# Even layer, tokens 512-1023: index scores, pooling, query rotation and attention placed beside the MLP of tokens 0-511, with raw projections kept until then

## The chip, the core and the metric

The kernel runs on one core of a Trainium2 chip. The metric is the device time in microseconds (us) of one execution; lower is better. The engines named below are TensorE (PE, the matmuls), VectorE (DVE), ScalarE (ACT), GpSimd (POOL) and SyncE (SP, which issues the DMAs).

## What is computed

Two layers over 1024 tokens of width 1024, in float32, and a final norm. The even layer mixes sparse attention (an indexer picks 256 causal keys for each query) with a pooling mixer; the odd layer is a gated delta rule. Each layer ends in a squared-ReLU MLP with 4096 hidden columns.

```python
for layer in range(2):
    hn = rmsnorm(h, mix_norm[layer])
    h = h + (sparse_pool_mixer(hn, ...) if layer % 2 == 0 else gated_deltanet(hn, ...))
    h = h + squared_relu_mlp(rmsnorm(h, mlp_norm[layer]), w_ff1[layer], w_ff2[layer])
return rmsnorm(h, final_norm)

def sparse_pool_mixer(h, ...):
    q, c_kv, qi, ki, wi, u = jnp.split(h @ w_in, ...)
    # q, qi, k, ki are rotated (rope); c_kv is normed; k = c_kv @ w_uk; v = c_kv @ w_uv
    ya = dsa_attention(q, k, v, qi, ki, wi)          # score = sum_h relu(qi . ki) * wi; top_k(score, 256)
    yb = multiscale_pool(u, pool_w, pool_scale)      # trailing means over 2, 4, 8, 16 tokens, minus the token
    return jnp.concatenate([ya, yb], axis=-1) @ w_out

def squared_relu_mlp(h, w1, w2):
    return jnp.square(jax.nn.relu(h @ w1)) @ w2
```

## The kernel before

Activations lie transposed in SBUF (128 channels by 512 tokens a tile), so the 1024 tokens are two halves, s = 0 and s = 1. The residual of half s is `h[s]`, eight tiles. A float32 product is made of three matmuls (`mm3`) on a high and a low part of each operand: every weight chunk (128 x 512) is loaded by SP into a `raw` buffer, copied by ACT to its high part (`copy`) and subtracted by POOL to its low part (`rest`). A chunk feeds 12 matmuls of 512 columns. The parts lie in rings of buffers, `W` (6 buffers before, that is three chunks) and `WM` (4); `room` says which rings a stream of chunks uses and how many chunks are prepared ahead. Stream "a" is the layers' projections, stream "m" the MLPs.

The program is written as Python generators and then ordered by a scheduler: each engine has one queue in program order, in which `high_priority(offset=n)` moves instructions forward.

The even layer (`even`) runs through these stages. First the projections of half 0 (`EVEN_A`: latent keys `ckv`, index keys `kiwi`, index queries `qi`, pooling `u`, queries `q`), with index scores, pooling and rotation right behind each (`late` generators). Then the projections of half 1 (`EVEN_B`), with attention of half 0 (`attend`, query blocks 0 to 3) and the index scores of half 1 (`index_scores`, blocks 4 to 7) taken in turns. Then the output projection of half 0 (`even_out`), the four query projections of half 1 and the norm of `h[0]` for its MLP (`normed`).

From there the MLP of half 0 is available as a filler: `mlp_half` is a generator whose steps are one up-projection (`project`, 24 matmuls, then `squared`) or one row of the down-projection (`accumulate`, 6 matmuls and one DVE addition to `h`). A group of 256 hidden columns is two of the first and eight of the second, 96 matmuls. `EARLY = 63` such steps are placed beside the selection of half 1, by `more(2)` per step of `topk`; the rest runs alone later (`alone`).

`topk` finds the 256th largest score of each query by 31 steps of bisection on the bits, four blocks at once. In a step DVE counts for blocks 4 and 5 (`L625`), ACT for blocks 6 and 7 (`L652`), and three small DVE instructions (`L664`, `L665`, `L650`) set the next candidate. Afterwards each block gets its mask (`L632`, `L625`, `L688` to `L693`, with a scan, `L690`, that writes to the ring `temps`). `attend` then makes, per block and pair of heads, scores on PE (`L364`), maximum on DVE (`L705`), exponentials on ACT, transposes on PE (`L726`), copies of these by DVE and ACT (`L728`) and the product with the values on PE (`L735`).

After attention of half 1 and `even_out(1)` the rest of the MLP of half 0 runs alone. The odd layer follows, and needs `h[0]` complete. The lines with a helper's number stand for many places: `L246` to `L248` are all `mm3`, `L175` all high parts, `L179` all low parts.

Of the kernel before, what the change touches and what calls it, by code (L numbers as in the profile page):

```python
# [34 lines left out]
EARLY = 63  # L35
# [99 lines left out]
class Trunk:  # L135
    def __init__(self, ctx, tc, I, out):
# [13 lines left out]
        self.H = [Ring(mp, f"h{n}", 8, 512) for n in range(2)]  # L150
        self.background, self.masked, self.pace, self.solo = [], {0, 1}, 3, False
# [75 lines left out]


# [307 lines left out]

    def even_query(self, s, p, ps):

        pc = self.swapped(ps)
        yield  # L540
        self.qs[s].append(self.query_stacks(pc, s, self.Q))

    def even_pool(self, s, g, ps):
# [9 lines left out]
        nc.vector.tensor_tensor(u[:, 16:528], ps, self.rb, op=OP.mult)  # L553
# [10 lines left out]
        pl = self.H[1].get()  # L564
# [16 lines left out]
    def even_steps(self, s, x, keys, first=()):  # L581
# [21 lines left out]
    def topk(self, blocks, nv):  # L603
# [29 lines left out]

        for g in range(G):
# [14 lines left out]
        for b in range(30, -1, -1):  # L649
# [16 lines left out]
            yield  # L666
        for g in range(G):
# [131 lines left out]
    def squared(self, ps, ring):  # L799

        nc = self.nc
        r, y = self.T.get(), ring.parts()
# [3 lines left out]
        nc.vector.scalar_tensor_tensor(ps, ps, 0.0, r, op0=OP.max, op1=OP.mult)  # L806
        self.rest(y[:, 512:1024], ps, y[:, 0:512], False)
# [21 lines left out]
    def mlp_half(self, l, s, x, ring):  # L829
# [5 lines left out]
        for g, n, before, chunks in self.mlp_order():  # L835
            if g is not None:
                ps = self.project(("f1", l, 2 * g + n), x, st="m")
                if n == 0:
                    a[g] = [self.squared(ps, ring)]
# [3 lines left out]
            if g is not None and n == 1:  # L843
                a[g].append(self.squared(ps, ring))
# [342 lines left out]
    def even_units(self):  # L1187
# [11 lines left out]
        second = EVEN_B.copy()  # L1199
        second.insert(second.index(("u", 0)) + 3, "pool")  # L1200
        return list(chain(*(u[k] for k in first + second))) + out + list(chain(*(u["q", p] for p in range(4)))) + out


    def even(self):
# [3 lines left out]
        with ExitStack() as st:  # L1208
# [12 lines left out]
            with ExitStack() as st3:  # L1221
# [18 lines left out]
                scores = chain(*(self.index_scores(1, p) for p in range(4)))  # L1240
                for _ in self.even_steps(1, x, EVEN_B):
                    take(att, 3)
                    take(scores)
                while self.late:
                    take(att, 3)
                    take(scores)
                    self.step_late()
                for _ in att:
                    take(scores)
                acc, done = None, 0  # L1250
                for _ in self.even_out(0, ya, self.yb[0], self.PB):
# [3 lines left out]
                    take(scores)  # L1255
                self.x0 = self.rb
                self.room("a", self.W)
                for n, _ in enumerate(self.even_steps(1, x, [("q", p) for p in range(4)])):
                    if n == 0:
                        acc = self.rstd_cols(acc, D)  # L1260
                    if n == 1:
                        self.copy(self.x0, self.over_partitions(acc))
                    if n == 3:
                        self.x0 = self.normed(self.h[0], R_MLP, self.x0)
                        break
# [164 lines left out]
```

## Time and profile before

| | |
|---|---|
| median of 3 runs | 2830.18 us (2829.31 to 2831.47) |
| profiled execution | 2833.8 us |
| its span, first to last instruction | 2832.0 us |
| PE busy | 2652.9 us (94%) |
| DVE busy | 1711.8 us (60%) |
| mean granted TensorE clock | 0.972 of full speed |

The span is what the profile shows; the profiled execution's own time is 1.8 us longer. Busy time is an average over the whole program; the stages differ.

### The profile page before, as it was taken

Reading aid. Unit: us, or ns where it says so; the run is one execution under the profiler, and the core shown is the slowest. Engines: PE = TensorE matmul, PEld = TensorE weight load, DVE = VectorE, ACT = ScalarE, POOL = GpSimd, SP = SyncE. Lnnn points to the kernel's source line nnn. Section 1 sums busy time; section 2 is a strip of 40 time slices with the busy share of each in tenths; the row PEclk is TensorE's granted clock in tenths of the full one; section 3 lists DMA queues with packets and bytes.
Section 4 is the critical chain, followed back from the end, with each engine's and each line's share of the span. In section 5 each row is a group of like instructions: output and inputs, shape, how many; then the busy total and the mean of one; then the engine's idle time right before and its main releaser. Section 6 shows DMA issues by size and latency. Waiting matters only on the chain. (4 is left out here: it accounts for less than half of the span.)

```text
span 2832.0 us, 44713 instructions
## 1 busy us (share of the span) xinstructions
PE 2652.9 (94%) x16648; PEld 2097.5 (74%) x16648; DVE 1711.8 (60%) x3657; ACT 1186.2 (42%) x2472; POOL 1240.4 (44%) x1070
## 2 busy tenths in 40 slices
PE   8878969979999899999999989899999999899998
PEld 6656747857788677787777767677777777688886
DVE  6898898475533546565665567755665644733334
ACT  4556767345333343343333344433433323433332
POOL 6653354401544444445444434444444434544442
PEclk9889979989999999999999999999999999999999
DMA  5221123300332222222222211122222222333332
GB/s 165 65 67 45 59 84 95 92 12 23 101 97 89 80 78 78 69 71 83 79 72 76 70 53 56 55 78 68 75 79 79 66 63 86 117 98 96 96 96 78
DMA packets 119916, 218.81 MB, mean 77 GB/s; under 512 B 13970, under 2 KB 15122, under 8 KB 119698
## 3 DMA queue, kind: packets, MB, share of 16 engines
q1 hardware_dynamic: 119698, 215.95, 24.7%
q8 instruction: 131, 2.15, 0.3%
q14 instruction: 87, 0.71, 0.1%
HBM read 207.51 MB, written 4.19 MB: 75 GB/s over the span
## 5 line engine op out<-in xcount | busy, mean ns | idle before, releaser
L179 POOL TENSOR_TENSOR wm<-raw,wm 128x512 fp32r<-128x512 f32 x422 | 557.3, 1322 | 798.3 <-ACT wm L175 780.4
L175 ACT ACTIVATE wm<-raw 128x512 fp32r<-128x512 f32 x422 | 264.9, 628 | 654.4 <-PE ps_g L247 319.0
L179 POOL TENSOR_TENSOR w<-raw,w 128x512 fp32r<-128x512 f32 x222 | 295.9, 1334 | 345.5 <-ACT w L175 316.8
L820 DVE TENSOR_TENSOR h<-ps_d,h 128x512 f32<-128x512 f32 x424 | 288.0, 684 | 140.9 <-PE ps_d L248 139.2
L806 DVE SCALAR_TENSOR_TENSOR ps_g<-ps_g,temps 128x512 f32<-128x512 f32 x128 | 89.2, 696 | 358.8 <-ACT temps L804 358.8
L246 PE MATMUL ps_g<-x,w 128*128 128x512 f32 x644 | 260.7, 405 | 9.0 <-ACT w L175 6.3
L247 PE MATMUL ps_g<-x,w 128*128 128x512 f32 x644 | 260.0, 404 | 9.3 <-POOL x L179 6.0
L246 PE MATMUL ps_d<-y,wm 128*128 128x512 f32 x628 | 257.7, 410 | 11.3 <-DVE h L820 10.0
L248 PE MATMUL ps_g<-x,w 128*128 128x512 f32 x644 | 259.0, 402 | 0.7 <-POOL w L179 0.7
L175 ACT ACTIVATE w<-raw 128x512 fp32r<-128x512 f32 x222 | 138.9, 627 | 288.0 <-PE ps_g L247 191.2
L248 PE MATMUL ps_d<-y,wm 128*128 128x512 f32 x628 | 249.9, 398 | 0.6 <-POOL wm L179 0.6
L247 PE MATMUL ps_d<-y,wm 128*128 128x512 f32 x628 | 250.4, 399 | 0.0
L246 PE MATMUL ps_g<-xb,wm 128*128 128x512 f32 x512 | 205.2, 401 | 12.1 <-DVE y L179 7.6
L248 PE MATMUL ps_g<-xb,wm 128*128 128x512 f32 x512 | 205.3, 401 | 10.1 <-POOL wm L179 9.9
L247 PE MATMUL ps_g<-xb,wm 128*128 128x512 f32 x512 | 204.3, 399 | 0.6 <-POOL xb L179 0.6
L925 DVE SCALAR_TENSOR_TENSOR qkvz<-temps,conv,qkvz 128x512 f32<-128x512 f32 x144 | 134.8, 936 | 105.0 <-ACT qkvz L923 103.8
L246 PE MATMUL ps_g<-x,wm 128*128 128x512 f32 x352 | 142.1, 404 | 19.5 <-ACT x L175 15.4
L246 PEld LDWEIGHTS ps_g<-x,w 128*128 128x128 f32 x644 | 123.7, 192 | 40.7 <-ACT w L175 6.3
L247 PEld LDWEIGHTS ps_g<-x,w 128*128 128x128 f32 x644 | 123.8, 192 | 39.6 <-POOL x L179 7.5
L246 PEld LDWEIGHTS ps_d<-y,wm 128*128 128x128 f32 x628 | 118.3, 188 | 41.9 <-DVE h L820 14.5
L248 PEld LDWEIGHTS ps_g<-x,w 128*128 128x128 f32 x644 | 123.6, 192 | 28.2 <-POOL w L179 1.8
L247 PE MATMUL ps_g<-x,wm 128*128 128x512 f32 x352 | 142.0, 404 | 1.8 <-DVE x L179 1.2
(430 smaller groups left out, 6108.2 us busy)
## 6 DMA issues: line engine op xcount, KB each, us to landing
raw<-in_w_dram SPq DMA_DIRECT2D x512, 256.0 KB, 2.6
raw<-in_woi_dram SPq DMA_DIRECT2D x128, 256.0 KB, 2.6
raw<-in_wei_dram SPq DMA_DIRECT2D x52, 256.0 KB, 2.8
raw<-in_weo_dram SPq DMA_DIRECT2D x32, 256.0 KB, 2.6
raw<-in_woo_dram SPq DMA_DIRECT2D x32, 256.0 KB, 2.7
h<-in_xt_dram SPq DMA_DIRECT2D x16, 256.0 KB, 3.2
at<-at SPq DMA_DIRECT2D x64, 64.0 KB, 2.0
out_dram<-temps SPq DMA_DIRECT2D x16, 256.0 KB, 2.2
```

The costliest lines, as they stand in the source:

```text
L175: self.nc.scalar.activation(out, in_, AF.Copy)
L179: eng.tensor_tensor(lo, full, hi.bitcast(F32), op=OP.subtract)
L246: mm(ps, wh, xh, start=start, stop=False)
L247: mm(ps, wh, xl, start=False, stop=False)
L248: mm(ps, wl, xh, start=False, stop=stop)
L806: nc.vector.scalar_tensor_tensor(ps, ps, 0.0, r, op0=OP.max, op1=OP.mult)
L820: nc.vector.tensor_tensor(h, ps, h, op=OP.add)
L925: nc.vector.scalar_tensor_tensor(acc, pin[:, j:j + 512], cw(j), acc, op0=OP.mult, op1=OP.add)
```

## The change

Half 1's projections are all made right behind one another. The pooling and query projections of half 1 are only copied out of PSUM to the ring `H[1]` (`even_kept`). Two of them (`HELD = 2`, q2 and q3) are made behind `even_out(0)`. Then the norm of `h[0]` follows and the MLP of half 0 starts. Beside it stand, in this order, the 16 steps of the index scores of half 1, pooling and rotation on the kept tiles, the steps of `topk`, and the attention of half 1. `beside(us)` hands out MLP steps by a nominal budget per step: `BESIDE` is 4.0 (scores), 3.4 (kept tiles and bisection), 2.2 (attention), 6.0 (masks). Its unit is that of `T_COLS = 5.6` and `T_ROWS = 1.4` per MLP step.

Smaller edits: `W` has 4 buffers instead of 6, a ring `wo` of 2 serves the odd layer's output weights, and from `even_out(0)` on stream "a" uses `W` alone with one chunk ahead. The scan of a mask writes to `junk2` instead of a `temps` buffer. `topk` has its priority only while it searches. All four instructions of `squared` have priority 100 (before, the two on ACT). Half 1's pooling multiplies on POOL instead of DVE.

```diff
 KEYS = ["ckv", "kiwi"] + [("qi", p) for p in range(4)]
-EVEN_B = KEYS[:2] + list(chain(*((("u", p), ("qi", p)) for p in range(4))))
+EVEN_B = KEYS + [("u", p) for p in range(4)] + [("q", p) for p in range(4)]
+HELD = 2
+BESIDE = (4.0, 3.4, 2.2, 6.0)
...
-        self.W, self.WM, self.raw = Ring(wp, "w", 6, 512), Ring(wp, "wm", 4, 512), Ring(wp, "raw", 4, 512)
+        self.W, self.WM, self.raw = Ring(wp, "w", 4, 512), Ring(wp, "wm", 4, 512), Ring(wp, "raw", 4, 512)
...
-    @urgent(50)
     def step_background(self, g):
-        return next(g, self)
+        with self.tc.high_priority(offset=50) if self.searching else nullcontext():
+            return next(g, self)
...
+    def even_kept(self, s, key, ps):
+
+        raw = self.H[1].get()
+        self.copy(raw, ps)
+        self.kept.append((key, raw))
+        yield
+
...
-        nc.vector.tensor_tensor(u[:, 16:528], ps, self.rb, op=OP.mult)
+        (g2 if s else nc.vector).tensor_tensor(u[:, 16:528], ps, self.rb, op=OP.mult)
...
-            g = late[name](s, *n, ps)
+            g = self.even_kept(s, key, ps) if s and name in "uq" else late[name](s, *n, ps)
...
-            eq, cum = junk[:, :n], self.T.get(U16, n)
+            eq, cum = junk[:, :n], junk2.bitcast(U16)[:, :n]
...
             nc.scalar.activation(r, ps, AF.Relu)
             nc.scalar.activation(y[:, 0:512], r, AF.Square)
-        nc.vector.scalar_tensor_tensor(ps, ps, 0.0, r, op0=OP.max, op1=OP.mult)
-        self.rest(y[:, 512:1024], ps, y[:, 0:512], False)
+            nc.vector.scalar_tensor_tensor(ps, ps, 0.0, r, op0=OP.max, op1=OP.mult)
+            self.rest(y[:, 512:1024], ps, y[:, 0:512], False)
...
-                scores = chain(*(self.index_scores(1, p) for p in range(4)))
-                for _ in self.even_steps(1, x, EVEN_B):
+                for _ in self.even_steps(1, x, EVEN_B[:-HELD]):
                     take(att, 3)
-                    take(scores)
-                while self.late:
-                    take(att, 3)
-                    take(scores)
+                for _ in att:
                     self.step_late()
-                for _ in att:
-                    take(scores)
+                self.room("a", self.W)
...
+                for _ in self.even_steps(1, x, EVEN_B[-HELD:]):
                     pass
+                x0 = self.normed(self.h[0], R_MLP, r)
+
+                self.act = self.PB
+                fill, due = self.mlp_half(0, 0, x0), 0.0
+
+                def beside(us):
+                    nonlocal due
+                    due += us
+                    while due > 0:
+                        due -= next(fill)
+
+                for p in range(4):
+                    for _ in self.index_scores(1, p):
+                        beside(BESIDE[0])
+                for (name, n), raw in self.kept:
+                    g = {"u": self.even_pool, "q": self.even_query}[name](1, n, raw)
+                    next(g)
+                    self.step_late()
+                    self.late.append(g)
+                    beside(BESIDE[1])
+                    self.tick(1)
+                while self.late:
+                    beside(BESIDE[1])
+                    self.tick(1)
+                    self.step_late()
...
-            more(12)
             while self.background:
-                more(2)
+                beside(BESIDE[1] if self.searching else BESIDE[3])
                 self.tick(1)
+            beside(BESIDE[3])
...
-                for _ in self.attend(range(4, 8), self.qs[1], pb, ya):
-                    more(2)
-                more(EARLY)
+                att = self.attend(range(4, 8), self.qs[1], pb, ya)
+
+                with self.tc.issue_after(self.last_matmul()):
+                    next(att)
+                for _ in att:
+                    beside(BESIDE[2])
...
-            self.room("o", self.W, ahead=0)
+            self.room("o", Ring(op, "wo", 2, 512), ahead=0)
```

Three places show what the scheduler makes of it. The line numbers are those of the kernel in question; most lines of the changed kernel stand a few numbers lower or higher.

First DVE in the bisection, one up-projection's stretch of it. Before (`L664` sets the bit, `L806` and `L179` are `squared`, `L820` is a row's addition to `h`):

```order
L664 TENSOR_TENSOR tk_keep<-tk_cnt,tk_top 128x4
L665 COPY_PREDICATED tk_cur<-tk_keep,tk_cand 128x4
L650 TENSOR_SCALAR tk_cand<-tk_cur 128x4
L806 SCALAR_TENSOR_TENSOR ps_g<-ps_g,temps 128x512
L820 TENSOR_TENSOR h_101<-ps_t,h_101 128x512
L179 TENSOR_TENSOR y<-ps_g,y 128x512
L820 TENSOR_TENSOR h_102<-ps_t,h_102 128x512
L625 TENSOR_SCALAR junk,tk_cnt<-mask_78,tk_cand 128x640
L820 TENSOR_TENSOR h_103<-ps_t,h_103 128x512
L625 TENSOR_SCALAR junk,tk_cnt<-mask_79,tk_cand 128x768
L664 TENSOR_TENSOR tk_keep<-tk_cnt,tk_top 128x4
L820 TENSOR_TENSOR h_104<-ps_t,h_104 128x512
```

After (`L669`, `L813` and `L171`, `L827` are the same instructions):

```order
L669 TENSOR_TENSOR tk_keep<-tk_cnt,tk_top 128x4
L670 COPY_PREDICATED tk_cur<-tk_keep,tk_cand 128x4
L655 TENSOR_SCALAR tk_cand<-tk_cur 128x4
L629 TENSOR_SCALAR junk,tk_cnt<-mask_78,tk_cand 128x640
L629 TENSOR_SCALAR junk,tk_cnt<-mask_79,tk_cand 128x768
L813 SCALAR_TENSOR_TENSOR ps_g<-ps_g,temps 128x512
L827 TENSOR_TENSOR h_97<-ps_t,h_97 128x512
L171 TENSOR_TENSOR probs<-ps_g,probs 128x512
L827 TENSOR_TENSOR h_98<-ps_t,h_98 128x512
L669 TENSOR_TENSOR tk_keep<-tk_cnt,tk_top 128x4
L670 COPY_PREDICATED tk_cur<-tk_keep,tk_cand 128x4
L827 TENSOR_TENSOR h_99<-ps_t,h_99 128x512
```

The make-up is alike. Over the whole bisection a group of 96 MLP matmuls (eight additions, `h_97` to `h_104`) goes with some five bits before and with five to seven after.

Second DVE behind the last bit, at the masks. Before, the scan of the first mask (`L690`, block 4) stands behind all of the MLP's early additions:

```order
L179 TENSOR_TENSOR y<-ps_g,y 128x512
L820 TENSOR_TENSOR h_101<-ps_t,h_101 128x512
L820 TENSOR_TENSOR h_102<-ps_t,h_102 128x512
L820 TENSOR_TENSOR h_103<-ps_t,h_103 128x512
L820 TENSOR_TENSOR h_104<-ps_t,h_104 128x512
L690 SCALAR_TENSOR_TENSOR temps<-junk 128x640
L806 SCALAR_TENSOR_TENSOR ps_g<-ps_g,temps 128x512
L691 SCALAR_TENSOR_TENSOR junk<-temps,tk_t_3888,junk 128x640
L179 TENSOR_TENSOR y<-ps_g,y 128x512
L693 SCALAR_TENSOR_TENSOR mask_78<-junk,score_86 128x640
```

After, the same scan (`L696`) stands some ten rows behind the end of the bisection, with MLP rows between the masks:

```order
L686 TENSOR_TENSOR tk_cur<-tk_cur,tk_sg 128x4
L636 TENSOR_SCALAR score_89<-score_89,tk_sg 128x1024
L629 TENSOR_SCALAR junk,tk_cnt<-score_86,tk_cur 128x640
L694 TENSOR_SCALAR tk_t_3984<-tk_cnt 128x1
L695 TENSOR_SCALAR junk<-score_86,tk_cur 128x640
L696 SCALAR_TENSOR_TENSOR junk<-junk 128x640
L698 TENSOR_SCALAR score_86<-score_86,tk_cur 128x640
L697 SCALAR_TENSOR_TENSOR junk<-junk,tk_t_3984 128x640
L813 SCALAR_TENSOR_TENSOR ps_g<-ps_g,temps 128x512
L699 SCALAR_TENSOR_TENSOR mask_78<-junk,score_86 128x640
```

The masks have moved forward, in front of the MLP rows that stood ahead of them.

Third PE in the attention of half 1, between two query blocks. Before, scores (`L364`), transposes (`L726`) and values (`L735`) follow one another:

```order
L364 MATMUL ps_t<-keys,q 128x128 x2
L726 MATMUL ps_t<-ca,probs_5184 128x128 x4
L726 MATMUL ps_t<-ca,probs_5196 128x128 x4
L726 MATMUL ps_t<-ca,probs_5184 128x128 x3
L735 MATMUL ps_o<-at,values 64x128
L726 MATMUL ps_t<-ca,probs_5184 128x128
L726 MATMUL ps_t<-ca,probs_5196 128x128 x2
L735 MATMUL ps_o<-at,values 64x128 x7
L726 MATMUL ps_t<-ca,probs_5196 128x128 x2
L735 MATMUL ps_o<-at,values 64x128
```

After (`L359`, `L732`, `L741`), 12 to 24 matmuls of the MLP (`L241` to `L243`) stand between the scores of one block and its transposes:

```order
L359 MATMUL ps_t<-keys,q 128x512 x2
L359 MATMUL ps_t<-keys,q 128x128 x2
L359 MATMUL ps_t<-keys,q 128x512 x2
L359 MATMUL ps_t<-keys,q 128x128 x2
L241 MATMUL ps_t<-probs,wm 128x512
L242 MATMUL ps_t<-probs,wm 128x512
L243 MATMUL ps_t<-probs,wm 128x512
```

Matmuls of the MLP have moved in where PE went from one block's scores straight on to its transposes.

## Rows read from the trace of the kernel before

**Rows 1.** The page: costliest groups (busy us, mean ns, idle before), and one of the DMA issues.

```profile
L179 POOL TENSOR_TENSOR w<-raw,w 128x512 fp32r<-128x512 f32 x222 | 295.9, 1334 | 345.5 <-ACT w L175 316.8
...
L246 PE MATMUL ps_g<-x,w 128*128 128x512 f32 x644 | 260.7, 405 | 9.0 <-ACT w L175 6.3
...
L175 ACT ACTIVATE w<-raw 128x512 fp32r<-128x512 f32 x222 | 138.9, 627 | 288.0 <-PE ps_g L247 191.2
...
at<-at SPq DMA_DIRECT2D x64, 64.0 KB, 2.0
```

**Rows 2.** Busy time by stretch: length, then each engine's busy us (instructions), clock, DMA.

```profile
219.00:316.00 97.00, 86.39 (x491) 63.13 (x492) 80.68 (x205) 69.48 (x160) 29.62 (x22) 0.98 0.13 39
316.00:362.00 46.00, 46.00 (x203) 37.73 (x202) 41.11 (x104) 38.94 (x71) 23.45 (x18) 1.00 0.28 92
362.00:426.00 64.00, 38.75 (x139) 29.21 (x137) 61.27 (x98) 37.13 (x66) 34.19 (x24) 0.76 0.26 79
426.00:502.00 76.00, 73.47 (x316) 58.88 (x316) 68.82 (x156) 53.35 (x97) 35.59 (x28) 1.00 0.32 97
...
572.00:600.00 28.00, 8.84 (x35) 6.29 (x33) 25.60 (x43) 5.64 (x12) 2.58 (x2) 0.63 0.06 19
600.00:690.00 90.00, 88.75 (x755) 69.58 (x755) 56.59 (x179) 53.02 (x98) 4.18 (x4) 1.00 0.01 1
690.00:932.00 242.00, 239.65 (x1053) 196.21 (x1052) 102.59 (x158) 86.65 (x145) 121.81 (x95) 1.00 0.31 95
```

**Rows 3.** Groups of DVE by line, 219 to 316 us.

```profile
L527 DVE SCALAR_TENSOR_TENSOR score<-ps_t,wi,score 128x512 f32<-128x512 f32 (+3 forms) x54 | 32.9, 648 | 2.7 <-ACT ps_t L522 2.6
...
L333 DVE TENSOR_TENSOR temps<-at,rope 128x512 f32<-128x512 f32 x3 | 2.0, 679 | 0.0
```

**Rows 4.** Groups of DVE by line, 426 to 502 us.

```profile
L625 DVE TENSOR_SCALAR_CACHE_REDUCE junk<-mask,tk_cand 128x640 bf16<-128x640 uint16 (+1 forms) x26 | 24.5, 943 | 0.6
L820 DVE TENSOR_TENSOR h<-ps_t,h 128x512 f32<-128x512 f32 x21 | 14.3, 681 | 0.0
L179 DVE TENSOR_TENSOR y<-ps_g,y 128x512 fp32r<-128x512 f32 x8 | 5.5, 684 | 0.2
...
L664 DVE TENSOR_TENSOR tk_keep<-tk_cnt,tk_top 128x4 f32<-128x4 f32 x14 | 4.6, 330 | 5.0 <-ACT junk L652 4.6
...
L650 DVE TENSOR_SCALAR tk_cand<-tk_cur 128x4 int32<-128x4 int32 x13 | 3.3, 257 | 0.4
L665 DVE COPY_PREDICATED tk_cur<-tk_keep,tk_cand 128x4 f32<-128x4 uint32 x14 | 2.3, 161 | 0.3
...
L669 DVE TENSOR_TENSOR tk_keep<-tk_cnt,tk_most 128x4 f32<-128x4 f32 x1 | 0.1, 149 | 0.0
```

**Rows 5.** Groups of DVE by line, 362 to 426 us.

```profile
L333 DVE TENSOR_TENSOR temps<-at,rope 128x512 f32<-128x512 f32 x4 | 5.9, 1480 | 0.0
L334 DVE TENSOR_TENSOR temps<-temps 128x512 f32<-128x512 f32 x4 | 5.8, 1458 | 0.1
...
L353 DVE TENSOR_TENSOR q<-temps,q 64x512 fp32r<-64x512 f32 x4 | 4.8, 1205 | 0.1
L352 DVE TENSOR_TENSOR q<-temps,q 64x512 fp32r<-64x512 f32 x4 | 3.7, 922 | 0.1
```

**Rows 6.** Groups of DVE by line, 97 to 150 us.

```profile
L650 DVE TENSOR_SCALAR tk_cand<-tk_cur 128x2 int32<-128x2 int32 x15 | 6.8, 454 | 0.4
```

**Rows 7.** Groups of PE by line, 362 to 426 us.

```profile
L246 PE MATMUL ps_g<-x,wm 128*128 128x512 f32 x12 | 6.9, 574 | 15.4 <-ACT x L175 15.4
```

**Rows 8.** Timeline of PE, 643.4 to 652 us: start, us, instructions.

```profile
647.77 1.30 PE L735 MATMUL ps_o<-at,values 128*64 128x128 f32 x18
649.00 1.08 PE L364 MATMUL ps_t<-keys,q 128*128 128x512 f32 x4
649.92 1.47 PE L726 MATMUL ps_t<-ca,probs 128*128 128x128 f32 x12
651.15 0.47 PE L364 MATMUL ps_t<-keys,q 128*128 128x512 f32 x1
```

More of the change, by code (lines that the diff above doesn't have):

```diff
@@ L226, in columns, with last_matmul @@
             yield [t.rearrange("p (k c) -> p k c", k=KT // 2) for t in self.chunk((key, n), st)]
+    def last_matmul(self):
+        return next(i for i in reversed(self.nc.cur_bb.bb.instructions) if i.engine == mybir.EngineType.PE)
     def tick(self, n=1):
@@ L483, in even_index_keys, with swapped @@
         self.wis.append(wi)
-    def swapped(self, ps):
-        pc = self.A.get()
-        self.copy(pc, ps)
+    def swapped(self, ps, raw=False):
+        pc = ps
+        if not raw:
+            pc = self.A.get()
+            self.copy(pc, ps)
         ps2 = self.A.get()
@@ L666, in topk @@
             yield
+        self.searching = G == 2
         for g in range(G):
@@ L796, in even_out, with squared @@
             yield
-    def squared(self, ps, ring):
+    def squared(self, ps):
         nc = self.nc
-        r, y = self.T.get(), ring.parts()
+        r, y = self.T.get(), self.act.parts()
+        self.acts.append(self.act)
         with self.tc.high_priority(offset=100):
@@ L838, in mlp_half @@
                 if n == 0:
-                    a[g] = [self.squared(ps, ring)]
+                    a[g] = [self.squared(ps)]
+                self.pending = n == 1
                 yield T_COLS
@@ L843, in mlp_half @@
             if g is not None and n == 1:
-                a[g].append(self.squared(ps, ring))
+                a[g].append(self.squared(ps))
+                self.pending = False
     def mlp_units(self, l):
@@ L1198, in even_units @@
         first.insert(first.index(("u", 0)) + 3, "pool")
-        second = EVEN_B.copy()
-        second.insert(second.index(("u", 0)) + 3, "pool")
-        return list(chain(*(u[k] for k in first + second))) + out + list(chain(*(u["q", p] for p in range(4)))) + out
+        units = lambda keys: list(chain(*(u[k] for k in keys)))
+        return units(first + EVEN_B[:-HELD]) + out + units(EVEN_B[-HELD:] + ["pool"]) + out
     def even(self):
@@ L1254, in even @@
                     done += 1
[L1255 to L1265, printed above, removed]
-                    take(scores, 2)
@@ L1270, in even @@
             wp = self.pool("early", stack=st, side="left")
             self.room("m", self.WM, Ring(wp, "wme", 4, 512))
-            fill = self.mlp_half(0, 0, self.x0, self.Y)
-            taken = 0
-            def more(n):
-                nonlocal taken
-                while n and taken < EARLY:
-                    next(fill)
-                    n, taken = n - 1, taken + 1
-                    if taken == EARLY - 8:
-                        self.room("m", self.WM)
-            more(12)
@@ L1290, in even @@
                 ya = []
-                for _ in self.attend(range(4, 8), self.qs[1], pb, ya):
-                    more(2)
-                more(EARLY)
-            for _ in self.even_out(1, ya, self.yb[1], self.PB):
-                pass
+                att = self.attend(range(4, 8), self.qs[1], pb, ya)
[3 more added lines that the diff above has]
+                    beside(BESIDE[2])
+            for _ in self.even_out(1, ya, self.yb[1], self.Y):
+                pass
+            self.room("m", self.WM)
+            self.act = self.Y
+            while self.pending or self.PB in self.acts or any(t[3] is not self.WM for t in self.ready["m"]):
+                next(fill)
         return fill
```

31 lines of the change are left out of this document (12 added, 19 removed).

## The prediction, made before the changed kernel ran

> **What bounds the kernel now.** I read the page first, for the costliest groups, then busy time by stretch, and then the groups of VectorE and TensorE inside the stretches that the change touches. The stretches are cut where the stages end: at 219 us the mask of block 3 is done, at 316 the output projection of half 0 begins, at 362 it ends, bisection of half 1 runs from there to about 570, its masks to 600, attention of half 1 to 690, and at 932 the MLP of half 0 is complete, which the odd layer waits for [rows 2]. Up to 932 four kinds of stretch can be seen. From 316 to 362 and from 690 to 932 PE is busy to 99 to 100%: these are bound by matmuls. From 362 to 426 VectorE is busy 61 of 64 us and PE 39, at a granted clock of 0.76. From 572 to 600 PE is busy 8.8 of 28 us, while VectorE makes the last masks. From 600 to 690 the page shows PE busy 89 of 90 us, but 755 small matmuls stand there, so I have to price them to see how full it is (below). What the change can win is therefore PE's idle time in the middle two kinds, and looseness in the last; the work itself stays.
>
> **The price of a matmul.** The stretch from 690 to 932 holds 1053 recorded matmuls in 242.0 us [rows 2]. By the program's order they are 1031 of 512 columns and a few small ones, so one costs 0.2347 us with its stalls; I take 0.228 where nothing stalls it (I subtract 3%; four scores of 512 columns beside it lie 0.23 us apart, 649.00 to 649.92 [rows 8]).
>
> **The change part by part**, as ends of stages, from 219.
>
> 1. Up to the mask of block 3. VectorE loses two poolings and gains rotations of index queries, about even; fewer steps stand in between: 216. Uncertain by 5 either way.
>
> 2. The rest of attention 0. Before, 219 to 316 also held 54 score additions on VectorE, 32.9 us [rows 3], and their matmuls. They leave. What stays is attention's small matmuls and 109 of 512 columns, in all some 46 us of PE work by the prices of 5 below; VectorE has 81 − 33 = 48 us [rows 2, 3]. Neither fills the stage, because blocks follow in a chain, so I take 80% of full PE: 58 us, to 274. Bounds: 52 (PE at 88%) and 69 (at 67%).
>
> 3. The output projection of half 0 takes 46 us before [rows 2]; with a chunk less ahead I add 2: 322.
>
> 4. q2 and q3 are 48 matmuls, 11 us. The norm of `h[0]` runs under them; before, PE stood 15.4 us for the norm's first product [rows 7], behind contended VectorE rows that have now gone later. I take 6 us of standing: 339. Bounds 2 and 15.
>
> 5. Scores of half 1, with 264 MLP matmuls beside them: 60 us, and 128 score matmuls of 128 to 512 columns, 22 us, with 6 for seams: 88, to 427. VectorE has about 73 us there (score additions at 0.648 [rows 3], 22 `L820` and the rest of `squared`), so PE bounds. By the bounds of these, 82 to 94.
>
> 6. The kept tiles, bisection and masks, with 684 MLP matmuls (7.1 groups of 96) beside them. PE needs 156 us. VectorE needs more, so I sum its rows. One bit is two counts and three small instructions, 2 × 0.943 + 0.330 + 0.161 + 0.257 = 2.63 us [rows 4]; 31 of them 81.7. One MLP group is eight additions of 0.681 and four instructions of `squared` near 0.684, 8.18 us; 7.1 of them 58.2 [rows 4]. Rotation of a query tile is 1.480 + 1.458 + 0.922 + 1.205 = 5.07 us; four of them 20.3 [rows 5]. VectorE's part of four poolings, about five instructions each at the 0.68 of a similar sum, is 13.6 [rows 3]. First counts in float32, the turn between the halves of the bits and the last counts are some 20 instructions of 1 us: 20. Masks: before, the stretch 572 to 600 held three of the four in 25.6 us, with some attention in it [rows 2]; I take 29 for four. Sum 223. Does such a sum give a time? In 426 to 502 the 24 groups, from the first at 24.5 to the last at 0.1, add to 77.0 in 76 us: records overlap a little and VectorE waits a little (5.0 us for ScalarE's counts), which cancels [rows 4]. So 222 us, to 649. PE idles 66 of it. If the clock falls to the 0.76 of 362 to 426, where PE was busy 61%, the 156 become 205, still under 222.
>
> 7. Attention 1 with 284 MLP matmuls. The matmuls of values lie 1.23 us for 18 apart, 0.068 (timeline, 647.77 to 649.00), transposes 1.23 for 12, 0.103 (649.92 to 651.15) [rows 8]. 416 of the first are 28 (25 where they run in a row), 224 of the second 23, 128 score matmuls 24: 73 to 76 of PE work, in 90 us before. With 65 for the MLP, 140; 6 of this lies under the last masks, seams of 3 are added: 137, to 786. Bounds 128 and 150.
>
> 8. The output projection of half 1 (192) and the 304 matmuls left, alone, at 0.2347: 116.4, to 902.4.
>
> So half 0's MLP is done at 902.4 instead of 932: 29.6 us sooner. The moved steps bring their DMAs along: each rotated tile has four 64 KB transfers of 2.0 us on SP's queue [rows 1], 16 in all, which now stand among the MLP's weight loads. They can wait there for a `raw` buffer, one chunk's time; behind them only rotation waits, and VectorE has bits' counts and MLP rows to do in the meantime. I cost that at nothing; without cover it would be 4 × 4 us. Poolings' multiplication on POOL is four instructions at about 1.33 [rows 1], on an engine busy 44%. The new priority of `squared` I cost at nothing, as VectorE is not the bound where MLPs run alone (103 of 242 us [rows 2]). The odd layer has the same matmuls; I take its length as unchanged, with 8 us either way.
>
> The profile's own time is 2833.8 us, 0.13% over the median 2830.18. 2833.8 − 29.6 = 2804.2, and by the same ratio a median of **2801 us**, with own range 2785 to 2818.
>
> **What one row says against the change.** The same rotation row `L333` took 0.679 us in 219 to 316 and 1.480 in 362 to 426 [rows 3, 5]; POOL was busy 30% of the first stretch and 53% of the second [rows 2]. Stage 6 puts rotations and poolings beside POOL's splitting of MLP weights, so I took the dear row for rotation and the cheap one for pooling; with both cheap the sum falls by 9.4, with both dear it rises by 16.
>
> The Trainium skill has a rule for it: "SBUF — State Buffer", section "Who interferes with whom", says that VectorE and GpSimd share one pair of ports, held by one instruction at a time, and that a VectorE instruction with two SBUF inputs blocks against a GpSimd instruction that reads SBUF, while one with a single SBUF input (outside two-port modes) does not. The trace agrees for `L333`, 0.68 against 1.48; `L820`, which reads PSUM and SBUF, stays at 0.681. By that rule alone the poolings would be dear too, the second of the two sums.
>
> **The rivals.**
>
> *VectorE is freer than I sum.* If rotation takes 0.68 a row (−9.4) and the small instructions of a bit the 0.16 of `L665` (−0.27 × 31 = −8), stage 6 is 205, and attention 0 at 88% saves 6: 23 less, **2778**. For it: stage 6 has MLP weights at a slower pace (684 matmuls in 222 us, against 316 in 76), so POOL splits less. Against it: ScalarE's counts, for which VectorE already waited.
>
> *VectorE is dearer, and the gain goes.* `L650` took 0.454 us in 97 to 150 against 0.257 [rows 4, 6]. At this ratio, 1.77, the three small instructions cost 0.57 × 31 = 18 us more, and dear poolings 16: stage 6 at 256, and the time is 2801 + 34 = **2835**, no change. For it: the new poolings and rotations stand next to bits. Against it: the stretch 426 to 502, the nearest in make-up, is where my prices are from.
>
> *The narrower ring makes PE wait (slower).* `W` falls from three chunks to two, and stream "a" has one chunk ahead through both output projections. A chunk takes 0.627 on ScalarE and 1.334 on POOL, 1.96 us, and PE uses it up in 12 × 0.228 = 2.73 [rows 1]. So 0.77 us is left for handing over and for ScalarE being late; one count of 1.1 us on ScalarE in front of a copy eats that. 222 chunks go through the ring in the whole program, the odd layer included. From 29.6/222 = 0.13 us a chunk the gain is gone; at 0.25 the time is 2801 + 55 = **2856**. For it: wait rows exist already (9.0 us at `L246` behind ScalarE's copy). Against it: that is 0.04 a chunk with six buffers, and the margin is positive where ScalarE has no counts.
>
> **How the numbers follow.** Chances: my sum 0.42, the freer VectorE 0.25, the dearer 0.17, the narrow ring 0.16. The range, 2768 to 2846, reaches from below the freer case, with the bounds of attention 1, through the dearer one to the ring at 0.2 a chunk. A change below 0.2% (5.7 us) can't be told from none. Faster: 0.40 + 0.25 + 0.05 = 0.70; same: 0.02 + 0.08 + 0.03 = 0.13; slower: 0.04 of the dearer and 0.13 of the ring, 0.17.
>
> **What would show it.** Right: the MLP's first matmul near 339; VectorE some 90% busy, as in 426 to 502, and PE near 70%, from 427 to 649; attention 1 with PE over 95% and near 137 us long; half 0's last addition near 902; the odd layer's length as before, 1857 us from the norm on. Wrong: rotations' rows at 0.68 (then earlier) or `L650` over 0.4 (then later) in stage 6; PE waits on `w` copies or rests in the output projections and the odd layer; a VectorE less than 85% busy in stage 6, which would mean that bits wait on ScalarE's counts and that my sum has the wrong engine.

## The result: slower by 36 us

The changed kernel takes 2865.42 us (median of 4 runs, 2861.59 to 2867.0); the kernel before took 2829.74 beside it. The ratio is 1.0126, 95% interval 1.0109 to 1.0144. Forecast were 2801 us, and a range of 2768 to 2846. The profiled execution took 2867.0 us, its span is 2865.2.

Busy time by stretch in the changed kernel, cut at the ends of the forecast's stages (length, then each engine's busy us and instructions, clock, DMA):

```profile
220.00:286.00 66.00, 62.51 (x377) 47.84 (x378) 29.13 (x109) 39.55 (x96) 17.00 (x13) 0.91 0.12 38
286.00:332.00 46.00, 46.00 (x219) 37.73 (x219) 12.29 (x16) 17.00 (x28) 23.25 (x18) 1.00 0.27 86
332.00:351.00 19.00, 16.54 (x73) 13.17 (x72) 14.14 (x26) 9.67 (x18) 11.19 (x8) 0.91 0.31 91
351.00:444.00 93.00, 89.39 (x389) 70.84 (x388) 63.99 (x115) 49.07 (x101) 37.19 (x29) 0.98 0.24 71
444.00:666.00 222.00, 181.48 (x719) 137.85 (x718) 208.62 (x407) 129.90 (x232) 105.59 (x77) 0.93 0.27 82
666.00:818.00 152.00, 149.74 (x1019) 119.02 (x1020) 84.78 (x234) 76.68 (x141) 32.20 (x25) 0.98 0.13 39
818.00:862.00 44.00, 44.00 (x195) 36.01 (x193) 5.95 (x9) 10.14 (x16) 20.70 (x16) 1.00 0.27 85
862.00:946.00 84.00, 76.72 (x320) 61.80 (x319) 45.43 (x77) 32.70 (x58) 37.13 (x31) 0.94 0.25 78
...
990.00:2865.00 1875.00, 1803.11 (x12524) 1424.42 (x12522) 1039.44 (x2220) 693.95 (x1536) 816.10 (x743) 0.99 0.25 77
```

| what ends | forecast | measured | the stage's own error |
|---|---|---|---|
| mask of block 3 | 216 | 220 | +4 |
| attention 0 (`even_out(0)` begins) | 274 | 286 | +8 |
| `even_out(0)` | 322 | 332 | -2 |
| q2, q3 and the norm of `h[0]` | 339 | 351 | +2 |
| index scores | 427 | 444 | +5 |
| masks of blocks 4 to 7 | 649 | 666 | 0 |
| attention 1 | 786 | 818 | +15 |
| `even_out(1)` and the MLP of half 0 | 902 | 946 | +12 |

Two things are to be seen. The longest stage, 444 to 666, came out at its 222 us: VectorE busy 209 of it, PE 181 by the profile and 164 by the prediction's price of 0.228 us for each of its 719 recorded matmuls. All the error of the even layer, 44 us, lies in shorter stages that were summed as if their parts fitted together. Half 0's MLP is ready some 15 us later than before: its last addition to `h[0]` begins at 948.0 instead of 933.0 (the cut at 946 lies about 1 us early). And the odd layer, which the prediction took as unchanged, takes 18 us more, 1875 instead of the 1857 of the kernel before:

```profile
975.00:2832.00 1857.00, 1790.65 (x12524) 1421.70 (x12523) 1041.64 (x2220) 690.77 (x1535) 815.00 (x742) 0.99 0.25 78
```

The even layer's 44 us and these 18 make 62 of the 64 us between the forecast and the measured time.

The odd layer's waits, as the view of waits lists them for PE from 990 us on (us in total, times, the longest):

```profile
PE ps_d L243 <- POOL wo L171: 21.6, 22, 3.1
...
PE ps_d L241 <- DVE h L827: 6.5, 7, 2.1
...
PE ps_d L241 <- ACT wo L167: 3.2, 6, 0.8
```

The first and the third name a ring that did not exist before, `wo` (`L167` and `L171` make a chunk's high and low part): 28 waits, 24.8 us. In the kernel before, where these weights went through `W`, the same wait is

```profile
PE ps_d L248 <- POOL w L179: 1.0, 2, 0.5
```

The end of the even layer, first by stretch, then as VectorE's timeline (start, us, instructions):

```profile
862.00:912.00 50.00, 49.62 (x218) 40.41 (x216) 19.61 (x31) 19.80 (x34) 22.25 (x18) 1.00 0.31 94
912.00:917.00 5.00, 1.83 (x9) 1.83 (x9) 2.91 (x4) 0.00 (x0) 0.98 (x1) 0.73 0.21 56
917.00:921.00 4.00, 4.00 (x11) 3.13 (x11) 1.96 (x12) 0.00 (x0) 0.00 (x0) 0.50 0.01 2
```

```profile
912.11 3.01 DVE L304 TENSOR_TENSOR temps<-temps 128x512 f32<-128x512 f32 x3
917.08 0.16 DVE L286 TENSOR_SCALAR rs_m<-ps_t 128x4 f32<-128x4 f32 x1 [1.96 <-PE ps_t L284]
...
919.25 0.16 DVE L265 SCALAR_TENSOR_TENSOR rs_y<-rs_t,rs_y 128x4 f32<-128x4 f32 x1
921.86 2.72 DVE L315 SCALAR_TENSOR_TENSOR temps<-h,prm,ps_t 128x512 f32<-128x512 f32 x4 [2.45 <-PE ps_t L272]
924.50 0.70 DVE L171 TENSOR_TENSOR xb<-temps,xb 128x512 fp32r<-128x512 f32 x1
```

From 862 to 912 PE is full. Then the squares of `h[1]` (`L304`) end at 915, PE stands (1.8 of 5 us busy), the reciprocal root runs through twelve small instructions to 919.4, and PE's granted clock is 0.50 from 917 to 921. The norm of half 1 stands open here. In the kernel before, the same rows lay right behind `even_out(1)`, from 728 on, with all of the MLP's rest behind them.

### The profile page after: what moved, and what is told of

It reads as the page before. It is cut to its first block, busy times and chain, and to the rows that moved or that the text cites. A ratio compares the mean times of both kernels' runs of the same rounds, so it can differ in the third digit from the quotient of the medians.

```text
span 2865.2 us, 44751 instructions
## 1 busy us (share of the span) xinstructions
PE 2678.5 (93%) x16648; PEld 2105.1 (73%) x16648; DVE 1711.5 (60%) x3653; ACT 1187.8 (41%) x2475; POOL 1248.2 (44%) x1074
## 5 line engine op out<-in xcount | busy, mean ns | idle before, releaser
L171 POOL TENSOR_TENSOR wm<-raw,wm 128x512 fp32r<-128x512 f32 x437 | 581.1, 1330 | 904.5 <-ACT wm L167 880.7
L167 ACT ACTIVATE wm<-raw 128x512 fp32r<-128x512 f32 x437 | 274.4, 628 | 690.7 <-PE ps_g L242 344.2
L171 POOL TENSOR_TENSOR w<-raw,w 128x512 fp32r<-128x512 f32 x196 | 259.1, 1322 | 310.2 <-ACT w L167 296.4
L827 DVE TENSOR_TENSOR h<-ps_d,h 128x512 f32<-128x512 f32 x392 | 266.6, 684 | 154.2 <-PE ps_d L243 152.2
L241 PE MATMUL ps_g<-x,w 128*128 128x512 f32 x648 | 265.0, 409 | 8.8 <-ACT w L167 7.2
L242 PE MATMUL ps_g<-x,w 128*128 128x512 f32 x648 | 263.7, 407 | 6.2 <-POOL x L171 4.0
L813 DVE SCALAR_TENSOR_TENSOR ps_g<-ps_g,temps 128x512 f32<-128x512 f32 x128 | 89.1, 696 | 300.7 <-ACT temps L811 300.7
L243 PE MATMUL ps_g<-x,w 128*128 128x512 f32 x648 | 263.3, 406 | 1.8 <-POOL w L171 1.8
L241 PE MATMUL ps_d<-y,wm 128*128 128x512 f32 x596 | 247.2, 415 | 7.6 <-DVE h L827 6.3
L242 PE MATMUL ps_d<-y,wm 128*128 128x512 f32 x596 | 238.9, 401 | 0.0
L243 PE MATMUL ps_d<-y,wm 128*128 128x512 f32 x596 | 238.5, 400 | 0.2 <-POOL wm L171 0.2
L167 ACT ACTIVATE w<-raw 128x512 fp32r<-128x512 f32 x196 | 122.9, 628 | 277.1 <-PE ps_g L242 208.4
L241 PE MATMUL ps_g<-xb,wm 128*128 128x512 f32 x512 | 204.7, 400 | 11.9 <-DVE y L171 7.6
L243 PE MATMUL ps_g<-xb,wm 128*128 128x512 f32 x512 | 204.4, 399 | 4.5 <-POOL wm L171 4.4
L241 PE MATMUL ps_g<-x,wm 128*128 128x512 f32 (+1 forms) x396 | 158.4, 400 | 6.1 <-ACT wm L167 4.7
L243 PE MATMUL ps_g<-x,wm 128*128 128x512 f32 (+1 forms) x396 | 157.7, 398 | 0.7 <-POOL wm L171 0.7
L242 PE MATMUL ps_g<-x,wm 128*128 128x512 f32 (+1 forms) x396 | 158.1, 399 | 0.0
L241 PEld LDWEIGHTS ps_g<-x,w 128*128 128x128 f32 x648 | 126.7, 196 | 41.1 <-ACT w L167 7.6
L242 PEld LDWEIGHTS ps_g<-x,w 128*128 128x128 f32 x648 | 126.0, 195 | 36.3 <-POOL x L171 5.3
L827 DVE TENSOR_TENSOR h<-ps_t,h 128x512 f32<-128x512 f32 x184 | 125.8, 686 | 42.4 <-PE ps_t L243 41.8
```

Of the source, the lines that this page charges most:

```text
L167: self.nc.scalar.activation(out, in_, AF.Copy)
L171: eng.tensor_tensor(lo, full, hi.bitcast(F32), op=OP.subtract)
L241: mm(ps, wh, xh, start=start, stop=False)
L242: mm(ps, wh, xl, start=False, stop=False)
L243: mm(ps, wl, xh, start=False, stop=stop)
L827: nc.vector.tensor_tensor(h, ps, h, op=OP.add)
```

## The experiments

Each is compared with the kernel before on the same chip; a difference between two kernels is that of their medians.

**e1, e2, e8: the rings.** e1 undoes one line of the change:

```diff
-            self.room("o", Ring(op, "wo", 2, 512), ahead=0)
+            self.room("o", self.W, ahead=0)
```

> The changed kernel with one line undone: the odd layer's output weights go through W again (now four buffers, two chunks), not through a ring of their own of one chunk. Theory A: the odd layer's extra 18 us (1875 against 1857) are PE's waits for that one-chunk ring, 21.6 + 3.2 us in the trace; they go, the odd layer takes 1857 to 1860 us, the time is near 2847. Theory B: the 18 us come from the odd layer's slightly different order or from the clock; the time stays at 2865.

Measured: 2887.55 us, ratio 1.0205 (1.0188 to 1.0222), 22 us slower still. The odd layer takes 1895 us. PE's waits from 930 us on:

```profile
PE ps_d L243 <- POOL w L171: 22.9, 24, 3.6
PE ps_g L243 <- POOL w L171: 10.4, 14, 1.4
```

With four buffers for both streams, the projections (`ps_g`) wait as well as the output (`ps_d`). So theory A had the right resource and the wrong remedy: what is missing is buffers in all, not a ring of its own. These two waits come to 33.3 us, 8 more than the change's waits for `wo` and `w`; they do not account for the whole 20 us by which the odd layer grew again.

e2 puts the same two lines into the kernel before:

```diff
-Ring(wp, "w", 6, 512)
+Ring(wp, "w", 4, 512)
-            self.room("o", self.W, ahead=0)
+            self.room("o", Ring(op, "wo", 2, 512), ahead=0)
```

> The kernel before with nothing changed but the rings: W of four buffers instead of six, and a ring wo of two for the odd layer's output weights. Theory A: the odd layer becomes 18 us longer, 2848, and the even layer stays within 3 us, because W's width was not what it waited for. Theory B: 2830, no change. If the narrower W itself made PE wait (the prediction's rival), the even layer would grow too, by 5 us or more.

Measured: 2851.66 us, ratio 1.0078 (1.0063 to 1.0093), 22.5 us slower than the kernel before. Its odd layer by stretch, and PE's wait for the ring:

```profile
976.00:2849.00 1873.00, 1798.00 (x12525) 1421.16 (x12523) 1042.84 (x2220) 694.04 (x1536) 817.44 (x743) 0.99 0.24 77
```

```profile
PE ps_d L248 <- POOL wo L179: 22.2, 22, 3.7
```

The last addition to `h[0]` begins at 935 there, against 933: the narrow `W` costs the even layer some 2 us, the rings of the odd layer 16 to 20.

e8 gives the changed kernel its old rings, with one `raw` buffer less to make room:

```diff
-Ring(wp, "w", 4, 512), Ring(wp, "wm", 4, 512), Ring(wp, "raw", 4, 512)
+Ring(wp, "w", 6, 512), Ring(wp, "wm", 4, 512), Ring(wp, "raw", 3, 512)
-            self.room("o", Ring(op, "wo", 2, 512), ahead=0)
+            self.room("o", self.W, ahead=0)
```

> The changed kernel with the weight rings of before: W of six buffers, and the odd layer's output weights through it; to find room, raw has three buffers instead of four. Theory A: the odd layer's 18 to 20 us go, 2846; the even layer stays, with at most 3 us less. Rival: a raw buffer less makes the loads late and takes back what the ring gives, 2860 or more.

Measured: 2844.89 us, ratio 1.0057 (1.0039 to 1.0075), 20.5 us faster than the change. The odd layer, which begins at 989.5:

```profile
989.50:2843.00 1853.50, 1791.30 (x12524) 1421.45 (x12522) 1039.19 (x2220) 691.25 (x1534) 814.62 (x742) 0.99 0.24 78
```

It is 1853.5 us, below the 1857 of before. e2 and e8 show theory A from both sides: the rings are worth 20 of the 36 us. Both runs change `W` and `wo` together; that the odd layer loses at `wo` and not at `W` is read from the waits (24.8 us against 0.5 in the change).

**e3: the mask's scan alone, in the kernel before.**

```diff
-            eq, cum = junk[:, :n], self.T.get(U16, n)
+            eq, cum = junk[:, :n], junk2.bitcast(U16)[:, :n]
```

> The kernel before with one line of the change: a mask's scan writes to junk2 instead of a buffer of temps. Theory C: the masks of blocks 4 to 7 were late only because the scan waited in the order for buffers that the MLP held; they are made beside the MLP before 572 us, and the idle 19 us of PE from 572 to 600 go: near 2811. Theory D: VectorE's 29 us of masks then delay the MLP's additions, or attention starts at the same time for another reason: 2825 to 2835.

Measured: 2822.68 us (10 runs), ratio 0.9975 (0.9966 to 0.9985): 6.4 us faster than the kernel before. Theory C holds for the place, and for a third of the size:

```profile
502.00:538.00 36.00, 27.59 (x103) 22.16 (x104) 35.69 (x46) 7.30 (x12) 14.97 (x8) 0.85 0.21 66
538.00:582.00 44.00, 44.00 (x188) 36.10 (x188) 15.35 (x24) 13.19 (x22) 18.07 (x14) 0.96 0.26 84
```

The masks are made from 502 to 538 beside the MLP, where VectorE is full and PE is busy 27.6 of 36 us, at a clock of 0.85; the 19 idle us of 572 to 600 [rows 2] are gone. VectorE's work did not shrink, so part of the idle time moved with it.

**e4: no MLP beside attention 1.** On top of e1:

```diff
-BESIDE = (4.0, 3.4, 2.2, 6.0)
+BESIDE = (4.0, 3.4, 0.0, 6.0)
```

> As e1_out_on_w, and the third number of BESIDE is 0: no MLP beside the attention of half 1, the 284 matmuls come behind it. The prediction's theory: MLP fills attention's gaps (137 us for both, against 90 and 65 apart), so that taking it away costs 18 us: 2865. Theory E: the two took 152 us together, which is their sum, and the MLP that is left covers the norm of half 1, whose chain from 912 to 946 stood open: 8 to 12 us faster than e1, near 2837.

Measured: 2890.82 us, ratio 1.0221 (1.0203 to 1.0239), against 2887.55 of e1: 3 us slower. The prediction's 18 us are not there, and theory E is wrong too. By stretch:

```profile
662.00:757.00 95.00, 91.65 (x759) 71.54 (x761) 62.13 (x201) 56.94 (x107) 3.85 (x3) 0.97 0.01 3
...
800.00:945.00 145.00, 138.96 (x600) 113.20 (x599) 71.21 (x113) 55.69 (x95) 70.32 (x55) 0.98 0.28 87
```

Attention alone took 95 us, the rest behind `even_out(1)` 145 instead of 84. Beside attention the change has 258 recorded MLP matmuls, 59 us at 0.228: 154 us apart against 152 together. If the growth of the rest, 61 us, is taken for their price, it is 156 against 152. So the overlap saves 2 to 4 us, not 18. The last addition to `h[0]` begins at 944.8, in e1 at 945.7; the 3 us between the medians lie in the odd layer of the profiles (1901 us from 987 on, 1894 from 988 on in e1). And the longer rest did not cover the norm: the same stand, 4.4 us in front of `L284`, came at 851, with half of the rest still to do, since the norm's rows stand behind the drained ones here too.

**e5: half 1's norm ahead of the drained MLP rows.** These are the MLP steps that the loop `while self.pending or ...` makes behind `even_out(1)`, until nothing uses the pools that close there.

```diff
+            self.r1 = self.rstd_cols(self.squares(self.h[1]), D, self.small(4, "r1", 1))
             self.room("m", self.WM)
             self.act = self.Y
             while self.pending or ...
...
-        x = self.normed(self.h[1], R_MLP, self.norm_scale(self.h[1]), XB)
+        x = self.normed(self.h[1], R_MLP, self.over_partitions(self.r1), XB)
```

> The changed kernel, with the sum of squares of half 1's norm put right behind its output projection, ahead of the MLP rows that are drained before the pools close. Theory: the 12 us that the stretch 862 to 946 takes over its 306 matmuls come from this norm, which stands in VectorE's order behind those rows (912 to 932), and from the clock that falls to 0.5 when PE stands; with the norm early they go: 2853. Rival: the 12 us are the end of a short remainder (nothing is left beside the last rows), and stay: 2865.

Measured: 2849.71 us, ratio 1.0072 (1.0057 to 1.0087), 15.7 us faster than the change. The two stretches behind attention:

```profile
818.00:862.00 44.00, 44.00 (x193) 36.13 (x193) 12.13 (x15) 14.55 (x23) 20.73 (x16) 1.00 0.27 87
862.00:936.00 74.00, 73.87 (x327) 59.84 (x327) 43.87 (x74) 31.43 (x53) 39.85 (x32) 1.00 0.27 88
```

PE is full from 818 to 936, at a clock of 1.00 throughout; the last addition to `h[0]` begins at 935.5 instead of 948, and the odd layer 13 us sooner. The loss came from where the norm stood in the order.

**e6: index scores beside attention 0 again**, the rest as changed:

```diff
+                scores = chain(*(self.index_scores(1, p) for p in range(4)))
                 for _ in self.even_steps(1, x, EVEN_B[:-HELD]):
                     take(att, 3)
+                    take(scores)
                 for _ in att:
+                    take(scores)
                     self.step_late()
...
-                for p in range(4):
-                    for _ in self.index_scores(1, p):
-                        beside(BESIDE[0])
+                for _ in scores:
+                    beside(BESIDE[0])
```

> The changed kernel, with the index scores of half 1 taken beside attention of half 0 again, as before; everything else stays. The 264 MLP matmuls that stood beside the scores then run later. Theory: the 66 us from 220 to 286 hold only some 51 us of matmuls, so scores fill 15 us of gaps; 93 us go, 60 come back later, attention 0 grows by 20: 13 us faster, 2852. Rival: attention 0 grows by the whole 33 us of score additions on VectorE: no change, 2865. The prediction had both cost the same.

Measured: 2842.25 us, ratio 1.0045 (1.0028 to 1.0062), 23.2 us faster than the change. By stretch:

```profile
221.00:312.00 91.00, 85.33 (x489) 63.85 (x489) 65.68 (x175) 63.18 (x151) 20.21 (x16) 1.00 0.09 30
312.00:362.00 50.00, 48.96 (x223) 37.86 (x220) 44.88 (x116) 39.17 (x70) 22.04 (x17) 1.00 0.26 85
362.00:564.00 202.00, 171.41 (x670) 130.66 (x669) 189.22 (x318) 110.36 (x196) 118.26 (x83) 0.92 0.28 89
...
778.00:924.00 146.00, 140.32 (x601) 114.32 (x600) 71.22 (x113) 54.96 (x94) 68.35 (x53) 0.96 0.27 84
```

Attention 0 with all scores takes 91 us instead of 66, 25 more for some 22 us of score matmuls on PE, so its gaps were hardly filled. The larger part is in the next row: with the scores done, the first bit is set at 323 instead of 468, and VectorE works on bisection through `even_out(0)`, 44.9 of 50 us. In the change VectorE is busy 12.3 of 46 us there, and in the kernel before 41.1 of 46 [rows 2]. So kept tiles, bisection and masks with q2, q3 and the norm take 202 us, against 19 + 222, though with fewer matmuls beside them (670 recorded against 73 + 719). I had forecast neither that gain nor its loss: my stage 3 counted PE alone.

**e7: more MLP beside the bits.** BESIDE (4.0, 4.6, 1.6, 6.0).

> The changed kernel with BESIDE (4.0, 4.6, 1.6, 6.0): 2.5 more groups of the MLP beside kept tiles, bisection and masks, 0.9 fewer beside attention, the others taken from the end. Theory, as in the prediction: stage 6 is bound by VectorE's rows; a group adds 8.2 us there and takes away 21.9 where PE alone bounds, 34 us faster: 2831. Rival: PE, busy 87% of 444 to 634, becomes the bound or the bits wait behind the MLP's rows; stage 6 grows by 18 to 22 us a group: 2855 to 2865.

Measured: 2847.58 us, ratio 1.0062 (1.0046 to 1.0078), 17.8 us faster than the change. By stretch:

```profile
444.00:643.00 199.00, 180.63 (x728) 140.08 (x727) 185.65 (x377) 131.60 (x236) 106.94 (x79) 0.96 0.30 92
643.00:682.00 39.00, 33.38 (x125) 26.33 (x124) 38.69 (x47) 9.65 (x16) 17.50 (x11) 0.87 0.24 73
...
866.00:927.00 61.00, 53.94 (x224) 43.05 (x223) 34.86 (x60) 25.31 (x45) 27.93 (x22) 0.92 0.21 66
```

Kept tiles, bisection and masks end at 682 instead of 666, for 840 recorded MLP matmuls instead of 697: 16 us for 1.5 groups, 11 a group, where I had 8.2; and the last row is 61 us instead of 84. The theory's direction holds, VectorE is still the bound there (busy 224 of 238 us); the number of groups moved was 1.5 and not the 2.5 that I had from the budget.

**e9 to e12: the edits together.** e9 is e5, e6 and BESIDE (4.0, 5.5, 2.2, 6.0). e10 adds e8's rings, e11 is e10 with 4.6 for 5.5, e12 is e10 with the change's BESIDE.

> The changed kernel with three edits together: half 1's norm early (e5: 16 us), its index scores beside attention 0 (e6: 23 us), and BESIDE's second number 5.5 (e7 with 4.6: 18 us). Theory: the three act at different places and add up, 2865 - 16 - 23 - 30 = 2796, faster than the kernel before although the odd layer's ring is still narrow. Rival: with 5.5 PE bounds the bisection's stretch, and less MLP is left to attention: 2815 or more.

> As e9, and the rings of e8. If all parts add up: e9 less 18, near 2778. If the raw buffer that is missing costs something beside the denser MLP: 2785 to 2800.

> As e10, with 4.6 for 5.5 in BESIDE. VectorE's rows bound the stretch at 4.6 (theory: 5 to 10 us slower than e10); if PE bounds it already at 5.5, the two are the same within 4 us.

> The changed kernel with e5's, e6's and e8's edits together and BESIDE as in the change: what is left of the change is the kept tiles, bisection, masks and attention beside the MLP. If the three act at separate places: 2865 - 16 - 23 - 20 = 2806, faster than the kernel before (2830) and than e3 (2823). If the early norm only moves its loss into the output projection, as the stretch 806 to 866 of e9 suggests (60 us for 213 matmuls): 2815 to 2822.

Measured: e9 2839.69 us, ratio 1.0034 (1.0023 to 1.0045); e10 2829.48, 0.9997 (0.9988 to 1.0006); e11 2827.59, 0.9984 (0.9973 to 0.9994); e12 2828.26, 0.9996 (0.9987 to 1.0005). They don't add up. Three rows of e9 show a part of why:

```profile
398.00:508.00 110.00, 93.96 (x378) 71.95 (x377) 103.41 (x192) 73.60 (x133) 61.84 (x47) 0.94 0.29 94
...
562.00:650.00 88.00, 87.90 (x387) 72.11 (x386) 35.20 (x55) 29.17 (x48) 41.31 (x32) 1.00 0.30 96
...
806.00:866.00 60.00, 53.09 (x236) 41.14 (x236) 16.58 (x29) 17.42 (x28) 21.23 (x17) 1.00 0.18 66
```

With its first bit set at 324, e9's bisection is over at 508, and the larger budget puts its matmuls behind the masks, 562 to 650, where PE is alone: no gain over e6. The last addition to `h[0]` begins at 924 in e6, in e9 at 923. The output projection of half 1 takes 60 us for 213 matmuls, for which the expectation of e12 blames the early norm. The trace names something else, a wait of PE once in each row of that projection:

```profile
PE ps_g L241 <- DVE h L801: 6.9, 8, 0.9
```

An up-projection of the MLP had ended at 791, and ScalarE read it out of its `ps_g` buffer only at 860, so one of the two `ps_g` buffers that the even layer has was taken throughout, and each row waited for the addition (`L801`) that empties the other. e10 has the same eight waits (6.8 us); e5, e6, e11 and e12 have none. This is read from the traces; no run took it away.

In e12, against e6, the early norm saves 3.5 us and not 13; and at 250 us, where only the rings differ (`raw` of three buffers), e12 is 5.7 us behind e6. e10 gains 10 us on e9 by the rings, not 18; e11 lies 1.9 us from e10, inside the 4 us that its expectation gave for a PE that bounds the stretch at 5.5 already. The rest of what is missing was not taken apart. With its three losses undone the change gains nothing that e12 could show, and of its forms none beats e3, which is the kernel before with one line of the change.

## Why the prediction was wrong, step by step

**"The odd layer has the same matmuls; I take its length as unchanged."** This step failed, by 18 us; shown by e2 and e8. The rival of the narrow ring was the right kind, with its price in the wrong place. I spread it over 222 chunks of `W`; it fell on the 32 of them that are the odd layer's output chunks, whose new ring `wo` holds a single one; the prediction has no term for that ring. Such a chunk can only be prepared when its predecessor is used up, so the margin of 0.77 us a chunk that I counted does not exist there and the 1.96 us of preparing [rows 1] stand partly open: 24.8 us over 28 waits, 0.9 each, 18 of it net. The prediction's own sign of this rival, PE's waits on weight copies in the odd layer, came true.

**Step 8, "alone, at 0.2347".** 128 us instead of 116.4, the norm of half 1, which the change moved behind drained MLP rows in the order. Shown by e5. I had priced the stretch by the mean of one in which this norm was hidden.

**Step 7, attention 1 with MLP: 137.** 152. e4 shows the mechanism wrong: little of attention's 90 us was gap that an MLP could fill. My price for its small matmuls (73 to 76 us) took the densest group of a timeline as the price of all; alone they take 95 us, and why they lie so far apart no run shows. The 6 us that I let lie under the last masks were only in part there, as PE stands just ahead of the cut at 666, from 659 to 666.4:

```profile
PE ps_t L359 <- DVE mx L711: 7.4, 1, 7.4
```

Block 4's mask is ready at 640, but VectorE's first row of attention stands in its order behind all four masks, at 666. That this order is the cause is read from the trace only; no run took it away.

**Steps 1 and 2.** 12 us late. By my own 46 us of PE work, PE is full to 70% and not to the 80% that I chose; that the chain from block to block is the reason is argued, not shown. 66 us lies within the bounds I gave (52 to 69). e6 shows that scores fill little of it.

**Step 5** was 5 us short, within its bounds; no run looked for the cause.

**Step 6 held to the microsecond**, partly by errors that cancel. VectorE's groups from 444 to 666:

```profile
L629 DVE TENSOR_SCALAR_CACHE_REDUCE junk<-mask,tk_cand 128x640 bf16<-128x640 uint16 (+3 forms) x62 | 58.5, 944 | 1.8
L827 DVE TENSOR_TENSOR h<-ps_t,h 128x512 f32<-128x512 f32 x57 | 38.6, 681 | 0.4 <-PE ps_t L243 0.3
L669 DVE TENSOR_TENSOR tk_keep<-tk_cnt,tk_top 128x4 f32<-128x4 f32 x31 | 12.3, 397 | 8.2 <-ACT junk L657 8.1
...
L565 DVE TENSOR_TENSOR temps<-temps 128x524 f32<-128x524 f32 (+2 forms) x6 | 8.4, 1396 | 0.4 <-POOL temps L565 0.4
...
L655 DVE TENSOR_SCALAR tk_cand<-tk_cur 128x4 int32<-128x4 int32 x30 | 6.1, 203 | 0.7
L670 DVE COPY_PREDICATED tk_cur<-tk_keep,tk_cand 128x4 f32<-128x4 uint32 x31 | 5.9, 191 | 0.9
...
L348 DVE TENSOR_TENSOR q<-temps,q 64x512 fp32r<-64x512 f32 x4 | 4.7, 1173 | 0.1
...
L329 DVE TENSOR_TENSOR temps<-temps 128x512 f32<-128x512 f32 x4 | 4.3, 1085 | 0.0
L569 DVE SCALAR_TENSOR_TENSOR h<-temps 128x512 f32<-128x512 f32 x4 | 4.3, 1074 | 0.0
...
L328 DVE TENSOR_TENSOR temps<-at,rope 128x512 f32<-128x512 f32 x4 | 3.4, 848 | 0.0
```

Counts and additions cost what [rows 4] said (0.944, 0.681). Bits' small instructions took 0.397 + 0.203 + 0.191 = 0.79 instead of 0.75. The rotation's rows `L328`, `L329` (before: `L333`, `L334`) took 0.848 and 1.085, between the 0.679 and 1.480 of [rows 3, 5], and VectorE waited 8.2 us for ScalarE's counts. The poolings' rows, `L565` and `L569`, were dear, 1.40 and 1.07 instead of 0.68, but they are ten and not the twenty that I counted: 12.7 us instead of 13.6. So neither rival about VectorE came true as a whole.

The Trainium skill's rule ("SBUF — State Buffer", section "Who interferes with whom") agrees in direction: five of the six rows of rotation and pooling with two inputs in SBUF stand above 0.68 here, with POOL busy 106 of 222 us, while `L827`, which reads PSUM and SBUF, stays at 0.681. The sixth, `L347`, took 0.685.

One reading of the kernel before was wrong as well: its bisection does not run from 362 to about 570. The first bit is set at 324 and the last at 482, and 11 of the 31 lie beside `even_out(0)`; in the change the first is set at 468. The two rows, of the kernel before and of the changed one:

```profile
323.85 0.16 DVE L664 TENSOR_TENSOR tk_keep<-tk_cnt,tk_top 128x4 f32<-128x4 f32 x1
468.15 0.15 DVE L669 TENSOR_TENSOR tk_keep<-tk_cnt,tk_top 128x4 f32<-128x4 f32 x1
```

This is no part of the forecast's error, since stage 6 was summed afresh, with all 31 bits, and held. It is a part of why the change gains nothing: the sum gave every stage its own bound and asked of none what the idle engine in it had been doing before. `even_out(0)` was PE's in both kernels, 46 us; in it VectorE's busy time fell by 29 us (41.1 to 12.3). A comparison with before, stage by stage and engine by engine, would have shown that the change gives away 29 us of cover on the engine that bounds its longest stage. Of what it gets in return, the overlap in attention 1 is worth 2 to 4 us; what the MLP beside kept tiles, bisection and masks is worth by itself was not measured, and neither were the new priority of `squared` and the pooling's multiplication on POOL.

## What to carry to other kernels

When work is moved to stand beside other work, ask for each engine what cover the moved work gave up: here the bisection's first bit went from 324 to 468 us, and with it VectorE's use of an output projection. Read the small edits of a change as carefully as its idea: a ring of one chunk cost 20 us and a norm that slipped behind drained rows 13 to 16, of a slowdown of 36. And gains of 16, 23 and 20 us, found one at a time, came to 37 together (e12), so run the sum before believing it.

## What was not expected of the hardware

A stand of PE of 3.6 us was followed by four us at a granted clock of 0.50, which is 1.2 GHz (917 to 921). The nine matmuls of 512 columns there began 0.43 us apart, and those behind them 0.23. Without the stand (e5) the clock stayed at 1.00 from 818 to 936. e4 shows the same once more, a stand of 4.4 us and then 0.50 from 852 to 856. So a short wait cost about half as much again after its end as while it lasted: nine matmuls at 0.20 us more each are 1.8 us.
